# Window probabilities in tiles of 256 and 384 columns, and score matmuls placed away from the borders of the attention units

## The chip, the cores and the metric

The kernel runs on one core of a Trainium2 chip. The metric is the device time of one execution in microseconds. Engines go by the profile's names: PE (TensorE, matmuls and transposes), PEld (its weight loads), DVE (VectorE), ACT (ScalarE), POOL (GpSimd), SP (SyncE, which issues most transfers).

## The reference

One layer of a decoder trunk on 1024 tokens of width 1024, float32, batch 1:

```
h   = RMSNorm(x)
[q | k/v per branch | branch gates | ret q,k,v,g | merge gates] = h @ W_in
A   = NSA(q, ...)    # compressed + selected + sliding-window attention
B   = retention(...)
x   = x + W_out( sigmoid(gA) * (A @ W_pA) + sigmoid(gB) * (B @ W_pB) )
x   = x + relu(RMSNorm(x) @ W_up)^2 @ W_down
y   = RMSNorm(x)
```

The attention has 8 heads of 64 in 2 groups and is computed per block of 128 queries. For each head three softmaxes are taken: over compressed keys (one per 16 tokens), over selected blocks of 64 keys (16 are selected, and there are 16, so that it is causal attention), and over a window of 512 keys. Each result is multiplied by its own gate, and the three are summed:

```
o = gate_c * softmax(q k_cmp) v_cmp + gate_s * softmax(q k_sel) v_sel + gate_w * softmax(q k_win) v_win
```

## The kernel before, in words

The stages follow one another: norm and projections, retention, then the attention with the matmuls of the merge gates mixed in, then merge, MLP and last norm. Matmuls are made from float32 numbers split into a high and a low part (`wh`, `wl`, `bh`, `bl`, `ph`, `pl`), so that one product is two or three matmuls. All matmuls pass through the helper `mm` (L164). The change is in the attention alone, some 357 to 734 us of the trace.

**Units.** A unit is a block of 128 queries `qb` (from 7 down to 0) and a group `g` of four heads: 16 units, numbered 0 to 15. A unit has two parts. `scores(n, qb, g, u)` goes through the four heads, first over the selected keys (`KKs`), then over window and compressed keys together (`KKw`). For each head and branch it makes score matmuls `S` into one of 4 PSUM tiles (pool `psS`), takes mask and row minimum on DVE (`smallest`, L1161), and the exponential with its row sum on ACT (`exponential`, L1165) into the SBUF tiles `pSa`, `pSb` (selected), `pW` (window) and `pC` (compressed). After two heads the factors (gate over row sum) are made on DVE (`factors`, L1211 to L1213), and POOL multiplies the probabilities by them in place (`weigh`, L1216). `pv(qb, g, u)` then goes over the blocks of 128 keys, selected ones first, window ones after, compressed ones ahead of the last: PE transposes the block for four heads into `pt` (L1303), ACT copies that to `ph` (L1304), DVE makes the rest `pl` (L1305), and PE sums the products with the values in `O`. At the end ACT copies half of `O` to a tile `gst` (L1316), and DVE writes the sum of both halves into `AT` (L1320), the attention's output in SBUF: 4 blocks of 1024 columns, one column per token. `AT`'s first columns belong to the last units.

Before, the window scores of a head lie in one `pW` tile of 640 columns, four of which exist; a window with its compressed keys is scored in two halves of nearly one width.

**Gate pieces.** Between all this PE works off the gate's matmuls. `gate_pieces` (L1044 to L1069) has 32 pieces of 8 steps of three matmuls into `gps` (`bh` with `wh`, `bl` with `wh`, `bh` with `wl`). Up to piece 16 all but piece 1 use the same PSUM bank (pool `psO`, one buffer), and piece 1 that of the transposes. After a piece's last matmul ACT evacuates the bank by a tanh into `gst` (L1067), and SP stores it. Two pieces share their weights; the split weights `wh` (ACT, L191) and `wl` (DVE, L194) of the next two are made by `gate_w` from inside a piece, into a ring of two buffers. `wh` has to keep its place in the program's order.

**What sets the order.** PE's order is written out by hand: `place` gives every step a position in units (n is the start of unit n), and all steps are sorted by it. `S_AT` holds the positions of the scores relative to the unit's start (from, to, and where the last weighing goes; selected, then window), `Q_AT` that of the preparation of a unit's queries (`QQ` on ACT, L1105, and `ql` on DVE, L1106), `C_AT` that of the copying of compressed keys into `KKw` (L1335), and `GATES` the number of gate steps per unit. The order on the other engines is made by a scheduler from that. A gate piece ends at each border between units and in the middle of each of the longer units.

## Time and profile before

| | |
|---|---|
| median of 3 runs | 1544.9 us (1543.25 to 1544.99) |
| profiled execution | 1543.7 us, of which the span of the trace 1541.5 us |
| granted clock of TensorE | 0.999 |
| PE busy | 1523.3 us, 99% of the span |
| DVE, ACT, POOL busy | 1038.4, 710.7, 515.1 us |

The prediction quotes lines of these views. The page lists busy time and instructions of each engine. The windows are a table with one row for a stretch of time: its length, then busy time and count for each engine, the clock, the share of DMA and its rate. The list of waits says which engine and line waited for which, with the sum in us, the number of waits and the longest. The timeline gives start, duration, engine, line and operands of each instruction, with the idle time before it and what ended it in brackets; neighbours of one kind are put together (x2). The lists by shape give busy time and mean duration (ns) of each shape of an instruction. The end of a matmul is modelled, so that records of consecutive matmuls overlap.

### The profile page before, as it was taken

The numbers are of one execution on the slowest core, as the hardware profiler recorded it, in microseconds if no ns is written. First come the engines' busy times: TensorE is split into PE (matmuls) and PEld (weight loads), VectorE is DVE, ScalarE is ACT, GpSimd is POOL, SyncE is SP. The second block draws the span as 40 slices with busy tenths as digits, with TensorE's granted clock in tenths as the row PEclk, the third lists the DMA queues.
The fourth block names the chain that finished last, engine by engine and source line by source line (L and its number), as shares of the span: only waits on it lengthen the run. The fifth ranks groups of instructions, "written<-read, shape, count | busy, mean of one in ns | idle before, by whom it ended". The sixth has DMA issues, their size and how long they took to land.

```text
span 1541.5 us, 21817 instructions
## 1 busy us (share of the span) xinstructions
PE 1523.3 (99%) x7529; PEld 1269.1 (82%) x7529; DVE 1038.4 (67%) x2000; ACT 710.7 (46%) x1574; POOL 515.1 (33%) x567
## 2 busy tenths in 40 slices
PE   9999999999999999999999999999999999999998
PEld 6888888898888787788888888888888888888887
DVE  6865661666778777775754378876666768786573
ACT  6653462555677667775421263222222244443452
POOL 4110011002233333333000014767777518723640
PEclk9999999999999999999999999999999999999999
DMA  5202215752111111111644433444444797573472
GB/s 207 90 18 65 59 45 131 210 173 69 55 42 36 62 42 42 63 62 63 232 137 157 138 127 104 151 150 150 151 151 151 245 342 262 199 250 123 143 276 93
DMA packets 101904, 202.85 MB, mean 132 GB/s; under 512 B 10714, under 2 KB 27490, under 8 KB 101730
## 3 DMA queue, kind: packets, MB, share of 16 engines
q1 hardware_dynamic: 100946, 199.30, 39.0%
q0 software_dynamic: 704, 1.90, 0.3%
q8 instruction: 59, 0.97, 0.2%
q14 instruction: 51, 0.42, 0.1%
q10 hardware_dynamic: 144, 0.26, 0.0%
HBM read 147.75 MB, written 53.61 MB: 131 GB/s over the span
## 4 chain that ended last, share of the span: by engine, by line
PE 87%; DVE 5%; ACT 3%; issue 3%; POOL 2%; DMA 0%; SPq 0%; POOLq 0%; ACTq 0%; DVEq 0%
PE mm L164 24%; PE mmu L164 21%; PE mmd L164 20%; PE gps L164 9%; PE O L164 3%; PE S L164 3%; PE pt L1303 3%; DVE pl L1305 1%; ACT pW L1165 1%; PE pc L164 1%; PE pO L164 1%; DVE S L1161 1%; ACT ph L1304 1%; PE tp L397 0%; PE pS L164 0%
## 5 line engine op out<-in xcount | busy, mean ns | idle before, releaser
L1460 DVE TENSOR_TENSOR wl<-raw,wh 128x1024 fp32r<-128x1024 f32 x134 | 218.7, 1656 | 88.7 <-ACT wh L1459 88.5
L1459 ACT ACTIVATE wh<-raw 128x1024 fp32r<-128x1024 f32 x134 | 136.6, 1054 | 156.0 <-PE mmd L164 100.1
L164 PE MATMUL mmd<-wl,wh 128*128 128x512 f32 (+1 forms) x464 | 177.2, 382 | 0.0
L164 PE MATMUL mmd<-wh 128*128 128x512 f32 (+1 forms) x464 | 177.2, 382 | 0.0
L164 PE MATMUL mmd<-wh,wl 128*128 128x512 f32 (+1 forms) x464 | 177.1, 382 | 0.0
L200 POOL TENSOR_SCALAR msq<-ssq 128x1 f32<-128x1 f32 (+1 forms) x32 | 7.7, 241 | 387.9 <-ACT h L206 223.3
L1161 DVE CUSTOM_DVE_ANT_0 S<-S,edge_m 128x512 f32<-128x512 f32 (+9 forms) x200 | 101.7, 516 | 32.9 <-PE S L164 27.7
L164 PE MATMUL mm<-wh,bh 128*128 128x512 f32 (+1 forms) x320 | 122.4, 382 | 0.1
L164 PE MATMUL mm<-wl,bh 128*128 128x512 f32 (+1 forms) x320 | 118.9, 372 | 0.4 <-DVE wl L499 0.4
L164 PE MATMUL mm<-wh,bl 128*128 128x512 f32 (+1 forms) x320 | 118.0, 373 | 0.0
L1305 DVE TENSOR_TENSOR pl<-pt,ph 128x512 fp32r<-128x512 f32 (+1 forms) x148 | 97.4, 660 | 25.3 <-ACT ph L1304 23.1
L164 PE MATMUL gps<-bh,wh 128*128 128x512 f32 x256 | 107.9, 421 | 0.0
L1304 ACT ACTIVATE ph<-pt 128x512 fp32r<-128x512 f32 (+1 forms) x148 | 85.2, 578 | 39.5 <-PE pt L1303 38.3
L164 PEld LDWEIGHTS mmd<-wh 128*128 128x128 f32 x464 | 87.2, 188 | 17.1
L164 PEld LDWEIGHTS mmd<-wh,wl 128*128 128x128 f32 x464 | 87.2, 188 | 17.0
L164 PEld LDWEIGHTS mmd<-wl,wh 128*128 128x128 f32 x464 | 87.2, 188 | 16.7
L164 PE MATMUL mmu<-bh,wh 128*128 128x512 f32 (+1 forms) x264 | 101.0, 383 | 0.0
L164 PE MATMUL mmu<-bl,wh 128*128 128x512 f32 (+1 forms) x264 | 100.9, 383 | 0.0
L164 PE MATMUL mmu<-bh,wl 128*128 128x512 f32 (+1 forms) x264 | 100.6, 383 | 0.0
L164 PE MATMUL gps<-bh,wl 128*128 128x512 f32 x256 | 100.6, 393 | 0.0
L164 PE MATMUL gps<-bl,wh 128*128 128x512 f32 x256 | 100.5, 393 | 0.0
L1216 POOL TENSOR_SCALAR pSa<-pSa,cf 128x512 f32<-128x512 f32 (+2 forms) x52 | 32.9, 646 | 133.7 <-DVE cf L1213 99.0
(381 smaller groups left out, 3999.2 us busy)
## 6 DMA issues: line engine op xcount, KB each, us to landing
raw<-u_scr SPq DMA_DIRECT2D x56, 512.0 KB, 4.4
raw<-w_down SPq DMA_DIRECT2D x41, 512.0 KB, 5.2
raw<-w_up SPq DMA_DIRECT2D x32, 512.0 KB, 3.9
u_scr<-u SPq DMA_DIRECT2D x60, 256.0 KB, 4.1
u_scr<-s SPq DMA_DIRECT2D x45, 256.0 KB, 2.3
y<-w_down SPq DMA_DIRECT2D x16, 512.0 KB, 7.0
x<-x SPq DMA_DIRECT2D x8, 512.0 KB, 4.8
raw<-w_ga SPq DMA_DIRECT2D x8, 512.0 KB, 3.9
```

The lines of the kernel that those rows point to most:

```text
L164: T.matmul(o, w, m, start=start, stop=stop)
L200: G.tensor_scalar(m[:, :w], ssq, 1.0 / n, EPS, op0=OP.mult, op1=OP.add)
L1161: return V.tensor_tensor_reduce(sc, sc, mk, -0.125, BIGPOS, OP.add, OP.min, mx[:, i, b:b + 1])
L1165: A.activation(o, sc, AF.Exp, bias=mx[:, i, m:m + 1], scale=-1.0, accum_out=sums[:, i, b:b + 1])
L1216: G.tensor_scalar(v, v, cf[:, i, b:b + 1], 1.0, op0=OP.mult, op1=OP.mult)
L1303: T.transpose(tp[:, k], ps[k if n == 2 else (0, 2, 1, 3)[k]], ident)
L1304: A.activation(ph[:, :n], tp[:, :n], AF.Copy)
L1305: V.tensor_sub(pl[:, :n], tp[:, :n], ph[:, :n])
L1459: A.activation(h[:, :n], r, AF.Copy)
L1460: V.tensor_sub(l[:, :n], r, h[:, :n])
```

## The change

The window's probabilities of a head lie in two tiles, `pX` of 256 columns and `pW` of 384, four each. In odd units up to 9 the second one is a piece of `AT` instead, whose first 384 columns are written only by the units of the last three query blocks. The score matmuls are cut accordingly, 256 columns and the rest (448 at most, with the compressed keys). POOL weighs the 256 columns of both heads first, then the 384 (two instructions where there was one). The shorter units use `pSa`, `pSb` and `pW` by a new rule. `S_AT` has new positions, by query block: in the longer units the window scores of heads 0 and 1 come ahead of the border between units, those of heads 2 and 3 behind it. `Q_AT` goes from 0.1 to 0.33, `C_AT` from 0.45 to 0.6, for the longer units.

```diff
-        [(-0.59, -0.18, -0.12), (-0.08, 0.24, 0.3)],
-        [(-0.62, -0.18, -0.12), (-0.09, 0.2, 0.25)],
-        [(-0.75, -0.4, -0.35), (-0.42, -0.05, 0.05)],
...
-C_AT = [0.45, 0.15]
-Q_AT = 0.1
+S_AT = {0: ([(-0.75, -0.25)], -0.18, [], 0), 1: ([(-0.75, -0.5)], -0.45, [(-0.45, -0.14)], -0.08),
...
+        4: ([(-0.6, -0.26)], -0.2, [(-0.22, -0.03), (0.09, 0.22)], 0.25),
+        5: ([(-0.58, -0.24)], -0.19, [(-0.21, -0.02), (0.09, 0.24)], 0.28),
...
+C_AT = [0.6, 0.15]
+Q_AT = 0.33
...
-            win_w = [cW] if cW <= 448 else [(cW + cC) // 2, (cW - cC) // 2]
+            win_w = [cW] if qb < 3 else [2 * P, cW - 2 * P]
...
+            def ptile(t):
+                return at.tile([P, {"pX": 256, "pW": 384}.get(t, 512)], F32, name=t, tag=t, bufs=PS_S)
...
+                names = ("pSa", "pSb") if qb > 3 else ("pSa",) if n in (8, 10, 13, 15) else ("pSb",)
+                sel.append([ptile(t) for t in names])
...
+                elif qb == 2:
+                    win.append([ptile("pSa" if n % 2 else "pW")[:, :cW]])
                 else:
-                    win.append(new(2)[0][:, :cW])
+                    win.append([ptile("pX"), (AT[:, i] if n % 2 else ptile("pW"))[:, :cW - 256]])
...
-                        o = win[i][:, c0:c0 + w]
+                        o = win[i][b // 2 - 1]
...
-                for i in (hp * 2, hp * 2 + 1):
-                    weigh(win[i], i, 2)
+                for e in range(len(win_w)):
+                    for i in (hp * 2, hp * 2 + 1):
+                        weigh(win[i][e], i, 2)
...
-            blocks += [(lambda c=slice(kb * P, (kb + 1) * P): [t[:, c] for t in u["win"]], Vw[:, w0 + kb, g])
-                       for kb in range(nw)]
+            ws = [(0, kb) if qb < 3 or kb < 2 else (1, kb - 2) for kb in range(nw)]
+            blocks += [(lambda e=e, c=slice(k * P, (k + 1) * P): [t[e][:, c] for t in u["win"]], Vw[:, w0 + kb, g])
+                       for kb, (e, k) in enumerate(ws)]
...
-                place(prep_q(qb, g), 1, n - 1 + Q_AT, n - 1 + Q_AT)
+                place(prep_q(qb, g), 1, n - 1 + (Q_AT if qb > 3 else 0.1), n - 1 + (Q_AT if qb > 3 else 0.1))
...
-            for k, (lo, hi, w) in zip(n_scores(qb), S_AT[min(n, 1 + (7 - qb))]):
-                place(it, k - 1, n + lo, n + hi)
+            sel, w_sel, win, w_win = S_AT[qb] if n else S_FIRST
+            for k, parts, w in zip(n_scores(qb), (sel, win), (w_sel, w_win)):
+                for lo, hi in parts:
+                    place(it, (k - 1) // len(parts), n + lo, n + hi)
```

The instructions of the other engines move too. On ACT, at the border of units 5 and 6, there stood before (the ending piece is `gps_6133`, its evacuation `gst_6276`; the exponentials read `S`, and the `gst` of a border reads `gps`):

```order
L1304 ACTIVATE ph_6225<-pt_6224 128x256
L1165 ACTIVATE pSa_6220,sums_6093<-S_6206,mx_6094 128x384
L1165 ACTIVATE pSb_6221,sums_6093<-S_6215,mx_6094 128x256
L1304 ACTIVATE ph_6247<-pt_6246 128x512
L1067 ACTIVATE gst_6276<-gps_6133 128x512
L1165 ACTIVATE pW_6267,sums_6093<-S_6255,mx_6094 128x340
L1165 ACTIVATE pW_6267,sums_6093<-S_6261,mx_6094 128x300
L1165 ACTIVATE pC_6268,sums_6093<-S_6261,mx_6094 128x40
L1304 ACTIVATE ph_6289<-pt_6288 128x512
```

At the same place stands now (the ending piece is `gps_6168`, its evacuation `gst_6328`; code above the attention is two lines shorter, and the attention's lines are three to five lower):

```order
L1301 ACTIVATE ph_6304<-pt_6303 128x512
L189 ACTIVATE wh_6469<-raw_6467 128x1024
L1160 ACTIVATE pX_6318,sums_6129<-S_6296,mx_6130 128x256
L1160 ACTIVATE pW_6319,sums_6129<-S_6312,mx_6130 128x384
L1160 ACTIVATE pC_6289,sums_6129<-S_6312,mx_6130 128x40
L1065 ACTIVATE gst_6328<-gps_6168 128x512
L1301 ACTIVATE ph_6337<-pt_6336 128x512
```

The weight split `wh` and three exponentials, which came behind the evacuation or later in the unit, now come ahead of it. The ends of units 0, 1, 2 and 3 have the same order of these instructions now, and so has the place ahead of unit 0; at the end of unit 4 there are three exponentials and no `wh` ahead, in the middle of unit 5 two exponentials.

On PE there stood at the same border, from the piece's last matmuls to the first one of the next piece:

```order
L164 MATMUL gps_6133<-bl_86,wh_5728 128x512
L164 MATMUL gps_6133<-bh_85,wl_5729 128x512
L164 MATMUL S_6279<-KKw_2792,QQ_5990 128x340
L164 MATMUL S_6279<-KKw_2792,ql_5991 128x340
L164 MATMUL O_5937<-pl_6226,Vc_2793 64x256 x2
L164 MATMUL O_5937<-ph_6225,Vc_2793 128x256 x2
L1303 MATMUL pt_6288<-ident_90,pSa_6108 128x128
L1303 MATMUL pt_6288<-ident_90,pSa_6188 128x128
L1303 MATMUL pt_6288<-ident_90,pSa_6151 128x128
L1303 MATMUL pt_6288<-ident_90,pSa_6220 128x128
L164 MATMUL gps_6297<-bh_85,wh_6077 128x512
```

And now:

```order
L162 MATMUL gps_6168<-bl_86,wh_5760 128x512
L162 MATMUL gps_6168<-bh_85,wl_5761 128x512
L162 MATMUL O_5979<-pl_6273,Vc_2793 64x256 x2
L162 MATMUL O_5979<-ph_6272,Vc_2793 128x256 x2
L1300 MATMUL pt_6336<-ident_90,pSa_6143 128x128
L1300 MATMUL pt_6336<-ident_90,pSa_6212 128x128
L1300 MATMUL pt_6336<-ident_90,pSa_6177 128x128
L1300 MATMUL pt_6336<-ident_90,pSa_6239 128x128
L162 MATMUL gps_6345<-bh_85,wh_6113 128x512
```

The score pair between the two pieces is gone from the border. The weights `wh_5760` of the ending piece lie in one of the ring's two buffers, and `wh_6469` is the next to be written there.

## The prediction

> **What bounds the kernel now.** I read the page first, then a table of TensorE's busy time by stage, then the list of TensorE's waits, then the timeline at the longest wait and at a border of two units. The page:

> ```profile
> span 1541.5 us, 21817 instructions
> PE 1523.3 (99%) x7529; PEld 1269.1 (82%) x7529; DVE 1038.4 (67%) x2000; ACT 710.7 (46%) x1574; POOL 515.1 (33%) x567
> ```

> TensorE sets the time. Where it idles is told by stage (columns: us; then busy time and instructions of PE, PEld, DVE, ACT, POOL; clock; DMA):

> ```profile
> 357.00:632.00 275.00, 267.21 (x1459) 219.55 (x1458) 211.08 (x725) 192.55 (x553) 95.98 (x170) 1.00 0.16 51
> ```

> The change touches only attention, from about 357 on. There 7.8 us (275.00 - 267.21) are idle in units 0 to 8, which hold nearly all of the waits below. Nothing outside the stage is fed earlier or later by it, so a wait won or lost here moves the end one to one. The waits:

> ```profile
> PE pt L1303 <- POOL pW L1216: 4.4, 6, 1.8
> PE S L164 <- ACT pSa L1165: 1.3, 2, 1.0
> ...
> PE S L164 <- ACT pW L1165: 0.8, 2, 0.4
> PE S L164 <- ACT pSb L1165: 0.6, 1, 0.6
> PE S L164 <- ACT pC L1165: 0.5, 1, 0.5
> PE O L164 <- DVE AT L1320: 0.5, 1, 0.5
> ```

> So the stage loses 4.4 us to transposes that wait until GpSimd has weighed the window probabilities, 3.2 us to score matmuls that wait for a PSUM tile, 0.5 us to one sum: 8.1 us in 13 waits. A matmul's record is about 0.39 us long while the next one starts 0.23 us later (first rows of the border below), so each wait costs 0.16 us more than the list says: 8.1 + 13 x 0.16 = 10.2 us. The longest, in unit 5:

> ```profile
> 529.09 1.06 ACT L191 ACTIVATE wh<-raw 128x1024 fp32r<-128x1024 f32 x1
> ...
> 530.04 0.55 ACT L1165 ACTIVATE pW<-S,mx 128x344 f32<-128x344 f32 x1
> ...
> 531.33 0.62 ACT L1304 ACTIVATE ph<-pt 128x512 fp32r<-128x512 f32 x1
> ...
> 532.93 1.57 POOL L1216 TENSOR_SCALAR pW<-pW,cf 128x640 f32<-128x640 f32 x2 [3.63 <-DVE cf L1213]
> ...
> 533.79 0.44 PE L1303 MATMUL pt<-ident,pW 128*128 128x128 f32 x2 [1.83 <-POOL pW L1216]
> ```

> The gate's weight split `wh` holds ScalarE for 0.95 us (529.09 to 530.04), three exponentials follow in 1.29 us (530.04 to 531.33), then the factors, then two weighings of 640 columns.

> The second place is the border of units 5 and 6, where a gate piece ends:

> ```profile
> 547.79 0.40 PE L164 MATMUL gps<-bl,wh 128*128 128x512 f32 x1
> ...
> 548.02 0.39 PE L164 MATMUL gps<-bh,wl 128*128 128x512 f32 x1
> 548.25 0.31 PE L164 MATMUL S<-KKw,QQ 128*128 128x340 f32 x1
> ...
> 548.45 0.60 ACT L1067 ACTIVATE gst<-gps 128x512 f32<-128x512 f32 x1 [1.12 <-PE gps L164]
> 548.56 0.39 PE L164 MATMUL O<-pl,Vc 128*64 128x256 f32 x2
> ...
> 549.38 0.48 PE L164 MATMUL gps<-bh,wh 128*128 128x512 f32 x1
> ```

> ScalarE has stood idle for 1.12 us and starts the evacuation `gst` 0.43 us after the last product's start. It ends at 549.05, and the next piece, which needs the same PSUM bank, starts at 549.38: 0.33 us to spare. Nobody waits here now.

> **The change part by part.**

> *Work.* The score columns stay the same (256 + 448 for 352 + 352 in the first units), so TensorE and VectorE gain and lose nothing. The exponentials by shape:

> ```profile
> L1165 ACT ACTIVATE pSb<-S,mx 128x256 f32<-128x256 f32 x16 | 7.5, 466 | 0.0
> ...
> L1165 ACT ACTIVATE pSa<-S,mx 128x384 f32<-128x384 f32 x8 | 4.7, 582 | 5.9 <-DVE mx L1196 5.8
> ...
> L1165 ACT ACTIVATE pW<-S,mx 128x340 f32<-128x340 f32 x8 | 4.3, 539 | 0.7 <-DVE mx L1196 0.6
> L1165 ACT ACTIVATE pW<-S,mx 128x300 f32<-128x300 f32 x8 | 4.0, 505 | 0.0
> ```

> 256 and 384 take 0.466 + 0.582 = 1.05 us, 340 and 300 took 1.04: nothing either. Where the second tile is the idle output buffer, the same engines write as many columns there: nothing.

> *The weighing.* GpSimd by shape:

> ```profile
> L1216 POOL TENSOR_SCALAR pW<-pW,cf 128x640 f32<-128x640 f32 x32 | 26.7, 847 | 70.2 <-DVE cf L1213 31.6 <-DVE mx L1196 13.7 <-PE gps L164 7.0
> ...
> L1216 POOL TENSOR_SCALAR pSb<-pSb,cf 128x384 f32<-128x384 f32 x16 | 9.2, 590 | 11.8 <-DVE cf L1213 10.2 <-ACT ph L1304 1.7
> ...
> L1216 POOL TENSOR_SCALAR pSb<-pSb,cf 128x256 f32<-128x256 f32 x16 | 7.5, 479 | 0.0
> ```

> A pair of heads cost 1.57 us before the first window block of all four heads could be turned; now two weighings of 256 columns, 0.96 us: 0.61 us sooner. The 384s (1.18 us more) are needed only two blocks later, with four products of a gate step or of O (0.23 us each) per block between. GpSimd's 40 extra instructions lie beside TensorE. And `wh` leaves the place ahead of these exponentials (0.95 us). Of the longest wait, 1.83 + 0.16 = 2.0 us, this leaves 2.0 - 0.61 - 0.95 = 0.4; the others fall under 0.3. Of 4.4 + 6 x 0.16 = 5.4 us I keep 1.0 (bounds: 0, and all 5.4). [...]

> *The score tiles.* Heads 0 and 1 have their window scores ahead of the border, heads 2 and 3 after it, none on it. The six waits for a PSUM tile (3.2 + 6 x 0.16 = 4.2 us) and the wait for AT (0.7) are nearly all just behind borders; I keep 0.8 (bounds 0 and 4.9), for the unit with the short window, whose new places are as crowded as the old. Together 1.8 of 10.2 us stays: a gain of 8.4.

> *The border.* With the new places ScalarE's order is another: at the ends of units 0, 1, 2, 3 and 5 `wh` and three exponentials stand ahead of `gst`. `wh` fills one of two buffers, and the buffer is free only when the ending piece has made its last product with the old weights, the row at 547.79. `gst` started 0.43 after the last product; so `wh` starts 0.43 after 547.79, at 548.22, and `gst` 0.95 + 1.29 later, at 550.46 instead of 548.45, and ends at 551.06. TensorE has one score pair less between the pieces (548.25 to 548.56, 0.31 us), so it comes to the next piece at 549.07. It waits until 551.06 + 0.03: **2.0 us**, five times: 10.1. Queued behind on ScalarE are `ph` and the `gst` of O, which TensorE needs only after the gate's step. Bounds: 1.07 each if `wh` costs nothing there, 2.5 if the late `ph` stops TensorE again.
> [...] Here the pieces share a bank; the row at 549.38 shows that 0.33 us of room made that harmless so far. [...] I go with the working above.

> With `wh` moves `wl` on VectorE, and SyncE's load of the raw weights ahead of both:

> ```profile
> L194 DVE TENSOR_TENSOR wl<-raw,wh x10: 1225/1226/1756, 358.4 to 614.2; 128x1024 fp32r<-128x1024 f32 x10
> ```

> Its 1.23 us now stand ahead of `pl` and AT, from the end of `wh` (549.17) to 550.4; TensorE itself is stopped until 551.09, so nobody waits, but without that cover an O would, by up to 0.5 as in the list. The load only waits for the same buffers' users; the late store of `gst` has no reader in this stage. The compressed keys' update, moved from 0.45 to 0.6 of a unit, waits on ScalarE for the unit's last window score and holds `QQ` and a head's exponentials; some 5 us of products lie between these and their first reader: nothing. `QQ` and `ql` move from 0.1 to 0.33, out of the crowded first part; that gain is in the waits for score tiles.

> *The three other places.* Ahead of unit 0 the same four instructions stand before `gst`. That piece lies in the bank of the transposes: the next user comes one gate step later (three products of 0.23, 0.69) but without the two pairs of O (half as wide, so like two whole products, 0.46): 2.0 - 0.2 = 1.8; as weighings are due there too I take 1.5. At the end of unit 4 only the three exponentials stand ahead: 1.29 less 0.4 that they may start earlier, 0.9. In the middle of unit 5 two exponentials (1.05 us), against some 0.3 of room and an early start: 0.4. From the sum: 10.1 + 1.5 + 0.9 + 0.4 = 12.9 us of new waits.

> *Sum.* 12.9 - 8.4 = **+4.5 us**. The profiled execution took 1543.7 (span 1541.5 and 2.2 around it), so 1548.2; the median of the runs is 1544.9, 1.2 above it, so **1549.4**.

> **The rivals.**
> *Faster: the border costs almost nothing.* If ScalarE could do `wh` and the exponentials in the 1.12 us that it idles ahead of `gst`, the borders would cost some 0.3 each (1.5) and the other places 0.4: 8.4 - 1.9 = -6.5, 1538.4. For it: that idle time, and the waits of the list, which the change does hit. Against: `wh` can't start in it, as its buffer is held by the very piece that ends. It decides if that buffer comes free a step earlier. [...] Chance 0.17.
> *No difference: `wh` is free, the exponentials aren't.* Each place with `wh` is 0.95 cheaper: five at 1.07, 0.55, 0.9, 0.4 make 7.2; 7.2 - 8.4 = -1.2, 1543.7. For it: `wh` waited for nobody at its old place; against it the same buffer. Chance 0.20.
> *Slower still: the weighing stays late.* Heads 2 and 3 get their window scores no sooner than before (until 0.24 of a unit behind the border in units 4 and 5, as now; until 0.20 behind it in units 8 and 9, where it was 0.05 ahead). If the exponentials of the stopped borders pile up ahead of theirs, the factors come as late as now, the 5.4 us of GpSimd's waits stay, and the change doesn't do what it says: +4.4 more, 1553.8. Against: after a stop of 2.0 us at the border TensorE's transposes are later too, and `wh` is gone from this chain. Chance 0.15.

> **How the numbers follow.** Forecast 0.48, the rivals 0.17, 0.20, 0.15. The forecast's own range, by the bounds of the border (down 2) and of the waits that stay (up 4), is 1546 to 1553.5. With the rivals, leaving out the outer half of the first and the top of the last: 1540 to 1556. A measurement here tells 0.2%, 3.1 us, from no change: 1541.8 to 1548.0 is the same. Faster: 0.17. Same: the second rival and a quarter of the forecast, 0.32. Slower: 0.51.

> **What would show it.** Right: in the list of TensorE's waits a new line, gate products that wait for ScalarE's `gst` (some 9 to 11 us, five waits of about 2), and POOL's line down to about 1. In the timeline at each of the five borders `wh`, three exponentials, `gst`, in that order, and `wh` starting within 0.1 of the end of the piece's second last product. Wrong: `gst` 0.43 after the last product as before (first rival); `wh` ended before it (second); POOL's line still above 4 (third).

## The result, and the profile after

The changed kernel takes 1556.35 us (median of 6 runs, 1556.17 to 1560.85), the one before 1544.1 us in the same series: 1.0084 times as long, 95% interval 1.0071 to 1.0097, some 12 us. Five of the six runs lie between 1556.17 and 1556.64 at a granted clock of 0.997; the sixth, 1560.85, has 0.994. 1549.4 was forecast, with a range of 1540 to 1556. The direction was right; some 12 us were lost where 4.5 were forecast.

The page of the changed kernel has as many instructions on TensorE as before, and a span 13.0 us longer:

```profile
span 1554.5 us, 21837 instructions
...
PE 1526.1 (98%) x7529; PEld 1271.5 (82%) x7529; DVE 1034.5 (67%) x2000; ACT 708.3 (46%) x1574; POOL 518.8 (33%) x607
```

TensorE's waits, by the same list as before (us in total, times, longest):

```profile
PE gps L162 <- ACT gst L1065: 12.2, 7, 2.2
PE S L162 <- ACT pX L1160: 2.2, 1, 2.2
PE pt L1300 <- POOL pX L1211: 1.7, 1, 1.7
PE pt L1300 <- ACT gst L1065: 1.6, 1, 1.6
...
PE S L162 <- ACT pC L1160: 0.5, 1, 0.5
```

The two lines on `gst` (13.8 us in 8 waits) are the new ones that the prediction named. Of the old ones nearly all are gone: GpSimd's 4.4 us in six waits, and all waits for score tiles but the 0.5 for `pC`. But two long ones have come that it did not name, 2.2 and 1.7 us; they lie in units 9 and 8. With the same 0.16 us per wait the list made 10.2 us before; now the five lines, 18.2 us in 11 waits, make 18.2 + 11 x 0.16 = 20.0.

The border of units 5 and 6, the place that the prediction worked out, in the timeline of after:

```profile
556.46 0.39 PE L162 MATMUL gps<-bl,wh 128*128 128x512 f32 x1
...
556.89 1.06 ACT L189 ACTIVATE wh<-raw 128x1024 fp32r<-128x1024 f32 x1
...
557.39 0.60 PE L1300 MATMUL pt<-ident,pSa 128*128 128x128 f32 x4
...
557.85 0.46 ACT L1160 ACTIVATE pX<-S,mx 128x256 f32<-128x256 f32 x1
...
559.12 0.60 ACT L1065 ACTIVATE gst<-gps 128x512 f32<-128x512 f32 x1
...
559.77 0.50 PE L162 MATMUL gps<-bh,wh 128*128 128x512 f32 x1 [1.78 <-ACT gst L1065]
```

`wh` starts 0.43 us after the piece's second last product and takes 0.96, the three exponentials take 1.27, and the next piece comes 2.03 us later than it could (557.39 and 0.35 for four transposes make 557.74). 2.0 was worked out.

In unit 8 (first row) and unit 9 (second row) TensorE stands for GpSimd and for an exponential:

```profile
621.12 0.78 PE L1300 MATMUL pt<-ident,pX 128*128 128x128 f32 x3 [1.71 <-POOL pX L1211]
...
641.56 0.40 PE L162 MATMUL S<-KKw,QQ 128*128 128x288 f32 x1 [2.24 <-ACT pX L1160]
```

And something that the trace of before doesn't have at all. In the stretches of 1 us (length, then busy time and count of PE, PEld, DVE, ACT, POOL, and the granted clock third from the end) the clock falls to half, twice:

```profile
407.00:408.00 1.00, 1.00 (x4) 0.79 (x5) 0.68 (x1) 0.28 (x1) 1.00 (x3) 0.82 0.84 115
408.00:409.00 1.00, 1.00 (x5) 0.73 (x4) 0.01 (x1) 0.27 (x1) 1.00 (x2) 0.50 0.77 184
...
411.00:412.00 1.00, 1.00 (x9) 0.85 (x8) 0.28 (x1) 0.46 (x1) 0.00 (x0) 0.97 0.00 0
...
622.00:623.00 1.00, 1.00 (x5) 0.78 (x4) 0.60 (x1) 0.60 (x1) 0.95 (x3) 0.84 0.00 0
```

(The two rows left out have 0.50 as well.) In the first stretch 0.18 + 3 x 0.50 + 0.03 = 1.7 us of clock are missing, in the second as much (0.84, three times 0.50, 0.95). PE counts as busy there (1.00 in the rows), so no list of waits shows it.

Together: 20.0 - 10.2 = 9.8 us of waits and 3.4 of slow clock make 13.2; the span grew by 13.0.

### The profile page after: what moved, and what is told of

Same layout as the page of the kernel before. It is cut to its first block, busy times and chain, and to the rows that moved or that the text cites. A ratio compares the mean times of both kernels' runs of the same rounds, so it can differ in the third digit from the quotient of the medians.

```text
span 1554.5 us, 21837 instructions
## 1 busy us (share of the span) xinstructions
PE 1526.1 (98%) x7529; PEld 1271.5 (82%) x7529; DVE 1034.5 (67%) x2000; ACT 708.3 (46%) x1574; POOL 518.8 (33%) x607
## 4 chain that ended last, share of the span: by engine, by line
PE 88%; DVE 4%; ACT 3%; issue 3%; POOL 1%; DMA 1%; SPq 0%; POOLq 0%; ACTq 0%; DVEq 0%
PE mm L162 23%; PE mmu L162 21%; PE mmd L162 20%; PE gps L162 10%; PE O L162 4%; PE S L162 3%; PE pt L1300 3%; PE pc L162 1%; PE pO L162 1%; DVE S L1156 1%; ACT pX L1160 1%; DVE pl L1302 0%; PE tp L395 0%; PE pS L162 0%; DMA raw<-w_r0a 0%
## 5 line engine op out<-in xcount | busy, mean ns | idle before, releaser
L1156 DVE CUSTOM_DVE_ANT_0 S<-S,edge_m 128x256 f32<-128x256 f32 (+3 forms) x200 | 101.9, 516 | 37.4 <-PE S L162 31.6
L162 PE MATMUL gps<-bh,wh 128*128 128x512 f32 x256 | 108.4, 423 | 12.2 <-ACT gst L1065 12.2
L1211 POOL TENSOR_SCALAR pSa<-pSa,cf 128x512 f32<-128x512 f32 (+3 forms) x60 | 36.6, 624 | 126.6 <-DVE cf L1208 89.4
```

Source lines behind the costliest of these rows:

```text
L162: T.matmul(o, w, m, start=start, stop=stop)
L1156: return V.tensor_tensor_reduce(sc, sc, mk, -0.125, BIGPOS, OP.add, OP.min, mx[:, i, b:b + 1])
L1211: G.tensor_scalar(v, v, cf[:, i, b:b + 1], 1.0, op0=OP.mult, op1=OP.mult)
```

## The experiments

Four theories stood open. **Borders**: what ScalarE has to do ahead of the evacuation of a gate piece stops TensorE (the prediction's). **Tiles**: the 40 more weighings and the probabilities in the output buffer cost the time. **Units 8 and 9**: their new places cost by themselves. **Clock**: the half-clock stretches follow from long stops.

One thing in the code was found first. `wh` is bound in the program's order to the instruction that was traced last on ScalarE. With `Q_AT` at 0.33 that is `QQ` of the next unit, traced just before `wh`; and `QQ`, whose input has long been there, is taken far forward by the scheduler, and no longer holds `wh` back. So the hypothesis, read from the code, was that one number moves `wh`.

### 1. Queries back to 0.1

```diff
-Q_AT = 0.33
+Q_AT = 0.1
```

> After with the next unit's query preparation back at 0.1 instead of 0.33, nothing else. The weight split wh was traced right behind QQ and is tied to it; with QQ elsewhere wh falls back to the middle of the unit and no longer stands ahead of the gate's evacuation at the borders and ahead of unit 0; three exponentials still do. Border theory: six waits shrink by the 0.95 us of wh, 5.7 us, and if they are then under about 2 us the half-clock stretch at 407 to 411 us goes too, 1.7 us: about 1549. Rival, the tiles themselves (40 more weighings, probabilities in the output buffer) cost the time: no change, 1556.

Measured: 1547.62 us, 1.0019 of before (1.0009 to 1.0028): 8.7 us less than the changed kernel, where 7.4 were expected. At the border of units 0 and 1 `wh` is gone; three exponentials still stand ahead of `gst`, and the next piece waits for it for 1.03 us, where the longest wait of after's list, 2.2, lay here:

```profile
404.48 0.63 ACT L1065 ACTIVATE gst<-gps 128x512 f32<-128x512 f32 x1
...
405.17 0.50 PE L162 MATMUL gps<-bh,wh 128*128 128x512 f32 x1 [1.03 <-ACT gst L1065]
```

and in the list of waits the line is down from 12.2 to

```profile
PE gps L162 <- ACT gst L1065: 4.3, 4, 1.2
```

So one number that looked like a detail made most of the loss, and the theory on tiles falls: they are all still there. The 8.7 us are not the price of `wh` alone, though: at the ends of units 3 and 5 and in the middle of unit 5 the exponentials are ordered otherwise too, and nobody waits for `gst` there any more. The waits in units 8 and 9 stay, and there is one half-clock stretch left in the profile, in unit 9.

The ten runs of this kernel fall into three groups: two near 1546.1 us at a granted clock of 0.999, four near 1547.5 at 0.998 and four near 1549.2 at 0.997. That fits none, one and two such stretches at 1.7 us each; the profiled run, 1547.59 with one, is in the middle group. So a median here can hang on how many stretches an execution catches.

### 2. Old places in units 8 and 9

```diff
-        2: ([(-0.7, -0.38)], -0.32, [(-0.3, -0.05)], 0.08), 3: ([(-0.7, -0.36)], -0.3, [(-0.28, -0.03), (0.07, 0.2)], 0.22),
+        2: ([(-0.7, -0.38)], -0.32, [(-0.3, -0.05)], 0.08), 3: ([(-0.75, -0.4)], -0.35, [(-0.42, -0.05)], 0.05),
```

> After with the old places of the scores for units 8 and 9 only (query block 3). Theory that these two units' late window scores cost by themselves: the waits of 1.9 us for GpSimd (unit 8) and 2.4 us for an exponential (unit 9) go, and the half-clock stretch at 622 to 626 us with them: 4.3 to 4.6 plus 1.7, about 1550. Rival, the waits in these units come from the new tiles: 1555 to 1557. The waits at the longer units' borders stay in both.

Measured: 1553.99 us (1.0064; 1.0047 to 1.0081), 2.4 us less than the changed kernel, not 6. The two waits are gone, as expected; the old ones of these places are back:

```profile
PE S L162 <- ACT pX L1160: 1.9, 3, 1.0
```

And the half clock is not gone, but elsewhere, 560 to 563 us, right behind the stop at the border of units 5 and 6, which in the changed kernel's profile had none:

```profile
560.00:561.00 1.00, 1.00 (x6) 1.00 (x5) 0.27 (x1) 0.63 (x2) 1.00 (x3) 0.50 0.75 225
```

The expectation was wrong in both: it took away a wait in a place that has another one behind it, and tied a slow stretch to its stop. The four runs lie between 1553.15 and 1556.66 at clocks of 0.998 to 0.996, so the 2.4 us are no sharp price.

### 3. The tiles alone

All positions as before (`S_AT`, `Q_AT`, `C_AT`), only the tiles changed.

```diff
-C_AT = [0.6, 0.15]
-Q_AT = 0.33
+C_AT = [0.45, 0.15]
+Q_AT = 0.1
...
-        5: ([(-0.58, -0.24)], -0.19, [(-0.21, -0.02), (0.09, 0.24)], 0.28),
...
+        4: ([(-0.62, -0.18)], -0.12, [(-0.09, 0.2)], 0.25), 5: ([(-0.59, -0.18)], -0.12, [(-0.08, 0.24)], 0.3),
```

> After with all positions of before (scores, queries, compressed keys): only the tiles of 256 and 384 columns, doubled in the output buffer, and the 40 more weighings are left of the change. Border theory: no evacuation of a gate piece is late, and GpSimd's waits fall from 5.4 to about 2 us: 1541 to 1544. Rival, the tiles cost the time: 1550 or more.

Measured: 1541.24 us, 0.9976 of before (0.9967 to 0.9985): faster by 4 us. GpSimd's line of 4.4 us in six waits is down to

```profile
PE pt L1298 <- POOL pX L1209: 2.3, 2, 1.5
```

and no line on `gst` is there. The tiles do what they are for. Not all of the 4 us is theirs: the two profiled executions differ by 2.2 us only (1541.48 against 1543.7). 17 of the 19 runs of before in this series took 1544.83 to 1545.44 at a granted clock of 0.997 to 0.998, and the other two 1543.85 and 1544.05 at 1.0. Against those two the tiles gain 2.7 us. The rest looks like a half-clock stretch that most executions of before have and the profiled one has not; no profile of a longer one was kept, so this is not shown.

### 4. The places alone

Before with the new positions and the new way to place them, probabilities in the tiles of 640.

```diff
+S_AT = {0: ([(-0.75, -0.25)], -0.18, [], 0), 1: ([(-0.75, -0.5)], -0.45, [(-0.45, -0.14)], -0.08),
...
+C_AT = [0.6, 0.15]
+Q_AT = 0.33
```

> Before with the new positions only, probabilities in the old tiles of 640 columns. In the order of ScalarE three exponentials, but not wh, stand ahead of the evacuation at six borders; ahead of unit 0 wh too. Border theory: about 1.1 at six borders, 1.8 and 1.1 at two other places, 4.6 + 1.7 in units 8 and 9, less some 5 of old waits for score tiles: about 1553, GpSimd's waits for pW 4 us or more. Rival, the tiles cost the time: 1544 or less.

Measured: 1560.1 us (1.0099; 1.0084 to 1.0114), worse than the whole change and than expected.

```profile
PE gps L162 <- ACT gst L1065: 8.9, 8, 1.4
PE pt L1301 <- POOL pW L1214: 4.4, 6, 1.3
PE S L162 <- ACT pSa L1163: 2.2, 1, 2.2
PE pt L1301 <- POOL pSb L1214: 2.1, 2, 1.9
PE pt L1301 <- ACT gst L1065: 1.6, 1, 1.6
```

The exponentials alone make eight waits of up to 1.4 us. In this run `wh` stands behind `gst` at the six borders, although `Q_AT` is 0.33 here too; so late queries don't put it ahead in every program, and what the tiles add to that is open. Units 8 and 9 have their 2.1 and 2.2 us with the old tiles too, so these waits come from the places. GpSimd's line makes 4.4 us as before, but in units 6 and 7 for the most part.

The miss of 7 us isn't one thing. The terms of the expectation add up to 10.8 us, not to the 8 of its "about 1553". The places on `gst` make 11.9 us with 0.16 per wait, where 9.5 were put; some 5 of old waits were to go, and with those for `AT` only 2.8 went; and there are two half-clock stretches, not one:

```profile
625.00:626.00 1.00, 1.00 (x5) 0.71 (x4) 0.70 (x3) 0.44 (x1) 0.00 (x0) 0.63 0.00 0
...
645.00:646.00 1.00, 1.00 (x5) 0.68 (x4) 0.89 (x6) 0.84 (x4) 0.00 (x0) 0.87 0.00 0
```

### 5. In the kernel before, only the queries late

```diff
-Q_AT = 0.1
+Q_AT = 0.33
```

(for the longer units, as in the change)

> Before with one number changed: the next unit's query preparation at 0.33 instead of 0.1 in the longer units. By the order of ScalarE that alone puts wh right ahead of the gate's evacuation at the ends of units 0 to 5, without the three exponentials. Theory that the place of wh hangs on QQ and that it holds the evacuation: the evacuation starts 0.7 us later at these borders (0.95 from 0.43 after the second last product, 0.23 before the last one), 0.33 of that is spare, so six new waits of 0.4: 2.4 us; against that wh no longer stands ahead of the exponentials of the long wait in unit 5 (up to 0.95 less there and in unit 4). 1545.5 to 1547.5, with lines of gate products that wait for the evacuation. Rival, wh at the border costs nothing without the exponentials: 1543 to 1544.5 and no such lines.

Measured: 1542.46 us, 0.9984 of before (0.9975 to 0.9993): faster, which neither theory had in its range. The place of `wh` is as forecast, here at the border of units 0 and 1:

```profile
400.64 0.39 PE L164 MATMUL gps<-bl,wh 128*128 128x512 f32 x1
...
401.06 1.06 ACT L191 ACTIVATE wh<-raw 128x1024 fp32r<-128x1024 f32 x1 [0.58 <-PE gps L164]
...
402.67 0.50 PE L164 MATMUL gps<-bh,wh 128*128 128x512 f32 x1 [0.18 <-ACT gst L1067]
```

The wait is small, as there are no exponentials and a score pair lies between the pieces. What was undervalued is the other side:

```profile
PE gps L164 <- ACT gst L1067: 1.4, 5, 0.7
...
PE pt L1303 <- POOL pW L1216: 0.9, 3, 0.3
```

GpSimd's line falls from 4.4 to 0.9 us, because `wh` no longer stands ahead of the exponentials in the middle of units 4 and 5. The same number that costs 8.7 us on top of the new places gains 2.7 on top of the old ones (1.7 against the eleven runs of before at a clock of 0.999, which this kernel's runs have at least; their median is 1544.15).

### 6. Window heads 0 and 1 earlier

On top of experiment 8 below:

```diff
-        5: ([(-0.58, -0.24)], -0.19, [(-0.21, -0.02), (0.09, 0.24)], 0.28),
+        5: ([(-0.58, -0.24)], -0.19, [(-0.32, -0.12), (0.09, 0.24)], 0.28),
...
```

(and likewise for the other longer units)

> After with the query preparation at 0.1, the old places for units 8 and 9, and the window scores of heads 0 and 1 ended at 0.12 of a unit ahead of the border instead of 0.02. Theory that the evacuation is late only because wh and exponentials stand ahead of it: with both out of its way at the borders the waits of 1.2 to 2.5 us there go, those in units 8 and 9 are as before (2.7 us): 1538 to 1541, below the tiles alone. Rival, any score close to the border fills ScalarE just the same: waits of 1 us stay at five borders, 1544 or more.

Measured: 1545.92 us (1.0008; 0.9999 to 1.0017). The theory fails here, and the rival's waits are seen:

```profile
PE gps L162 <- ACT gst L1065: 5.4, 7, 1.1
```

The scores came earlier, but in ScalarE's order the exponentials of both heads, at most borders with a `ph` behind them, still stand right ahead of `gst`. Here an earlier place on TensorE doesn't clear the border on ScalarE, where the scheduler puts the order together.

### 7. The changed kernel again

> The changed kernel as it is, once more. If the half-clock stretches depend only on the length of the stop ahead of them, they come again at 407 to 411 and 622 to 626 us. If they hang on how the stop lies in a window of about 3.4 us that runs on its own (the two stretches begin 215.0 us apart, 63 windows of 3.413 us), they come at other stops of about 2 us, or in another number, and the time differs by 1.7 us for each.

Measured: 1556.53 us. Again two half-clock stretches, but in other places, and each 3.4 us long:

```profile
439.00:440.00 1.00, 1.00 (x5) 0.71 (x4) 0.69 (x1) 0.02 (x1) 1.00 (x3) 0.66 0.94 119
...
442.00:443.00 1.00, 1.00 (x7) 0.79 (x5) 0.70 (x2) 0.04 (x1) 0.00 (x0) 0.64 0.15 57
...
640.00:641.00 1.00, 0.79 (x4) 0.69 (x5) 0.11 (x1) 1.00 (x8) 0.00 (x0) 0.85 0.00 0
```

The start can be read from the first row of each: at 0.66, 0.68 of that microsecond ran at half clock, so it began at 439.32; the second at 640.70. The distance is 201.38 us, 59 times 3.413. In the first profile the starts are 407.64 and 622.68: 215.04 us, 63 times 3.413 (215.04 / 63 and 201.38 / 59 both give 3.413). The two stretches of experiment 4 start at 625.26 and 645.74, 20.48 us or 6 times 3.413 apart. By the rows a stretch itself lasts 3.42 us (0.36 + 3 + 0.06 in the first profile), and the clock entries of that trace give 3.413 for each of its two. So in each of the three profiles the two starts lie a whole number of stretch lengths apart, and a stretch costs half its length, 1.7 us. Why they lie so is not shown.

How the stops ahead of the stretches differ from the others can be counted in a trace, as an estimate, since the ends of matmuls are modelled. Lay pieces of 3.413 us out from the first entry of the granted clock in the first profile; the two stretches fill one piece each. Take 0.23 us for a matmul of 512 columns, less in proportion for fewer, 0.43 instead at half clock, and 0.09 for a transpose (0.35 for four), and add up in each piece the time in which TensorE stands still. Without the first and last 12 us these are 447 pieces. The two right ahead of the stretches have the most, 2.56 and 2.21 us; the next have 2.08, 2.04 and 1.93, and full clock behind them. In the trace of before, laid out in the same way, the most is 1.78, and none of them has half clock behind it. The length of a single stop does not sort them: the one ahead of 621.12 (1.9 us) is followed by half clock, the one ahead of 641.56 (2.24 + 0.16 = 2.4 us), which lies across two pieces, is not. With durations some 4% (or 0.02 for a transpose) off, the sums move by up to 0.1 us, but their order stays.

### 8. Queries at 0.1 and old places in units 8 and 9

The edits of experiments 1 and 2 together.

> After with the query preparation at 0.1 and the old places for units 8 and 9; heads 0 and 1 stay where after has them. The exponentials alone stand ahead of the evacuation: waits of 1.2 to 1.5 us at four borders as in the first experiment, in units 8 and 9 the 2.7 us of before instead of 4.6, and no half-clock stretch as no stop reaches 2 us: 1543.5 to 1545. The difference to the run with earlier heads is the price of the exponentials, 4 to 5 us by the border theory, 0 to 1 by its rival.

Measured: 1544.04 us (0.9993; 0.9984 to 1.0002), as expected, and without half clock; the longest wait for `gst` in its list is 1.2 us, as in experiment 1. The border's line on `gst` is the same as in experiment 1, word for word. The difference to experiment 6 has the other sign than expected (-1.9 us): the earlier heads are no way to price the exponentials.

### 9. One score pair back on the border

On top of experiment 8, for all longer units:

```diff
-        5: ([(-0.58, -0.24)], -0.19, [(-0.21, -0.02), (0.09, 0.24)], 0.28),
+        5: ([(-0.58, -0.24)], -0.19, [(-0.21, 0.01), (0.09, 0.24)], 0.28),
...
```

> The last experiment but one of after (queries at 0.1, old places in units 8 and 9) with one more change of places: the window scores of heads 0 and 1 end at 0.01 of a unit behind the border instead of 0.02 ahead, so that head 1's second score pair comes behind the gate piece's last product, as one pair did before. ScalarE's order then has the evacuation ahead of head 1's exponentials at every border. Theory that the exponentials ahead of the evacuation are what is left of the border's price: the lines of gate products waiting for the evacuation (4.3 us, four stops of 1.2 to 1.5) go, about 5 us: 1538.5 to 1540. Rival, the piece waits for another reason there, the transposes or the number of tiles: 1543 or more.

Measured: 1544.32 us (0.9994; 0.9985 to 1.0003), no gain. The line on `gst` is gone, as the theory had it, and a new one stands in its place:

```profile
PE O L162 <- DVE AT L1317: 3.4, 4, 1.0
```

A gate step later at the border of units 0 and 1:

```profile
406.98 0.85 DVE L1317 TENSOR_TENSOR AT<-O,gst 64x256 f32<-64x256 f32 x2 [0.24 <-ACT gst L1313]
...
407.97 0.47 PE L162 MATMUL O<-ph,VV 128*128 128x512 f32 x1 [0.99 <-DVE AT L1317]
```

The three exponentials now come behind the gate's `gst` and ahead of that of `O`; the next unit's `O` has the same PSUM tile and waits for its sum. Most of the 4.3 us was not won but handed on, and GpSimd's line is up to 1.9 us in 2 waits from 0.3 in one.

### 10. The tiles alone, with late queries

Experiment 3 with `Q_AT = 0.33`, a combination of the two gains (3 and 5).

> The tiles alone (all places of before) with the query preparation at 0.33, so that wh stands right ahead of the evacuation, without exponentials, at six borders. The fifth experiment's price and gain on the new tiles: about 0.4 at each of four to six borders lost (2 us), GpSimd's two waits of 1.0 and 1.6 us in units 4 and 5 gone since wh no longer stands ahead of those exponentials (2.3 us): 1540.5 to 1541.5, the same as the tiles alone. Rival, wh ahead of the evacuation is the whole of the border's price: 6 x 2, 1551 or more.

Measured: 1540.36 us, 0.9968 of before (0.9956 to 0.9981), just below the expected range, the lowest median of all and faster than both kernels.

```profile
PE O L160 <- DVE AT L1315: 1.3, 3, 0.6
...
PE gps L160 <- ACT gst L1063: 1.0, 2, 0.7
```

GpSimd's line is gone altogether; `wh` ahead of `gst`, without exponentials and with a score pair on the border, costs 1.0.

## Why the prediction was right and wrong

*What bounds the kernel* was right: changes in attention's waits are changes of the end (9.8 us of waits and 3.4 of clock against 13.0 of span).

*The border* was right in mechanism, place and price: 2.03 us where 2.0 was worked out. That the pieces share a PSUM bank cost nothing at this border before, with 0.33 us to spare; now the next piece waits 2.03 us for the bank's evacuation. The whole term was some 2 us too small: 12.2 + 1.6 in the list and 0.16 for each of 8 waits make 15.1, and 12.9 was the sum. The five borders with `wh` make 10.8 instead of 10.1: others are longer than this one (2.2 in the list, where this border's row has 1.78 idle). At the border of units 0 and 1 `wh` starts 0.87 us after the second last product, right behind a `ph`; that such a `ph` does it at all of them is not shown. The place at the end of unit 4 measured 1.4 for 0.9, the one in unit 5 1.2 for 0.4, the one ahead of unit 0 1.8 for 1.5. The reason given, that `wh` waits for the ending piece's products, is in the row of `wh` in experiment 5 (0.58 us, ended by `gps`), and that it is paid by TensorE is what experiment 1 shows. What the prediction didn't see is why `wh` had moved at all (`Q_AT`, in this program); it read the order, which was enough for the price.

*The weighing and the score tiles* were right in size for the longer units, and only partly in mechanism. Of the 10.2 us of old waits only 0.7 is left, that for `pC`. But the places of the scores, to which the prediction gave the gain at the score tiles, are not what won it in the longer units: experiment 3, with the old places, already lacks their two waits for `pW` (0.8 us, in units 2 and 3, some 6 us behind a border and not just behind it, as the prediction reads them), and experiment 10, with the old places, lacks GpSimd's line as well. Three of the six waits for a tile (1.9 us) belonged to the scores of units 8 and 9 and were exchanged for longer ones. What the places did win is the wait for `AT` (0.7), which experiment 3 still has and experiment 1 has not. Two weighings in place of one shorten GpSimd's line, as the prediction worked out from its rows (experiment 3: 4.4 to 2.3 us).

*The step that failed* is the term "I keep 0.8 ... for the unit with the short window, whose new places are as crowded as the old". They are more crowded: the window scores of heads 2 and 3 come 0.07 to 0.20 of a unit behind the border, and 2.2 + 1.7 us with 2 x 0.16, 4.2 us, are waited there (the 1.7 for GpSimd, for which the weighing had kept 1.0 in all). The positions were read for the third rival and not priced; experiment 4 shows that the places do it, experiment 2 that the old ones cost 2 us of their own.

*What was in no step* is the clock: 3.4 us, because half clock came behind two stops, of 2.5 and 1.9 us, at 1.7 each. The prediction held the granted clock fixed without giving a reason; the trace of before has no such stretch.

So 4.5 became 13.0 by +2.2 (borders), -0.3 (the old waits elsewhere: 0.7 left where 1.0 was kept for GpSimd), +3.4 (units 8 and 9: 4.2 for 0.8) and +3.4 (clock): 13.2. The range ended too low, at 1556, because the two largest terms were missing in the same direction.

By the count of experiment 7 the clock's two cases differ too. The stop of 2.0 us behind 557.74 lies almost wholly in one piece of the first profile, which stands still for 2.08 us in all, and the clock stayed. The one ahead of 621.12 is only 1.9 us, but with the smaller gaps behind it its piece has 2.21, and the clock fell. The 2 us that the expectations of experiments 1 and 8 take as a limit for a stop were the author's estimate; no run shows such a limit.

What stays open: why `wh` stands behind `gst` in experiment 4, and what the later copying of the compressed keys (`C_AT`) does by itself, which no run shows.

## What to carry to other kernels

When a change moves matmuls, read what it does to the order of the engine that empties PSUM: what was put ahead of an evacuation whose bank is needed next was paid here beyond the room that was there (2.03 us at the border of units 5 and 6, where 0.33 had been to spare), and moving it behind that may only hand the wait to the next reader of the same engine (experiment 9: 3.4 us in 4 waits for `AT`, where `gst` had 4.3). Price a move in each place where it lands: the same number, `Q_AT`, lost 8.7 us beside one set of places and gained 2.7 beside another. And test the parts of a change apart: here the tiles gained 4 us and the late queries gained beside the old places; the new places, alone and with the late queries, hid both.
